# Last four k steps of the output ordered by token half, sums of squares on GpSimd, and two more quads with seven products in the ssm branch

## The chip, the core and the metric

The kernel runs on one core of a Trainium2 chip. The metric is the device time of one execution in microseconds (us). The core has five engines with instruction streams of their own: TensorE (PE, the matmuls), VectorE (DVE), ScalarE (ACT), GpSimd (POOL) and SyncE (SP), which here only issues transfers. Each engine executes its stream in the order in which it is written; semaphores make one wait for another.

## The reference

A hybrid layer on 256 tokens of width 2048, batch 1, in float32:

- `hn = rms_norm(x)`, then one wide projection `hn @ w_in` that is split into q, k, v, the gates, and the inputs of a state space branch (ssm).
- an attention branch with 16 heads and three dilated windows, gated, times `w_attn_branch`
- an ssm branch: a short causal convolution, a chunked scan, a gate and a norm give `y` (256 x 4096), which is multiplied with `w_ssm_branch` (4096 x 2048)
- `merged = sigmoid(g_a) * (o_a @ w_attn_branch) + sigmoid(g_s) * (y @ w_ssm_branch)`, then `x + merged @ w_out` and a last rms norm over each token's 2048 values.

The change touches two of the products, `y @ w_ssm_branch` and `merged @ w_out`, and the last norm.

## The kernel before

**Matmuls.** Each float32 operand is split into a high part (h) and a low part (l), and a product of two is made of three matmuls that add up in one bank of PSUM: high by high, high by low, low by high. Such a triple is one `triple` in `gemm_pair` (lines 375 to 378). All weights arrive as units of 128 x 1024 from one array, `wall`, in the order of use: 480 loads of 512 KB on SP's queue, into four buffers (`w`). For each unit ScalarE copies the high part (L220) and DVE subtracts to get the low part (L221); h and l have four buffers each.

**gemm_pair** (lines 361 to 444) makes a product of all 256 tokens with 1024 columns of a weight. Tokens lie in two halves (i = 0, 1) of 128 and columns in two halves (c = 0, 1) of 512, so there are four accumulators, es[2i + c], of one PSUM bank each. The loop runs over *quads*: a quad is two k tiles of 128 (so 2 x 2 blocks of x by 2 x 2 blocks of the weight). A plain quad takes eight triples: for both k, both i, both c. For the quads listed in `S_QUADS` a Strassen-like scheme takes seven triples in their place. It needs

- four combinations of the weight blocks, made on DVE (t13 at L421, w at L426 and L427) and each split again (L414 on ScalarE, L415 on DVE): in all, 7 DVE operations where a plain quad has 2;
- combinations of the blocks of x, made by `turn_x` (lines 341 to 359): DVE adds and subtracts (L347, L349 to L352) in a scratch tile and splits the results into high (L228, ScalarE) and low parts (L230, DVE). These are made once for a quad and used by both halves of the columns;
- four more banks, `prods` (pp in the profile), whose sums over all such quads are combined at the end by `fold` (L451 to L456) and added to the accumulators.

The second half of the columns (c = 2) uses the eight banks with the roles exchanged (`swap`): its accumulators take the banks of the first half's prods, its prods those of the first half's accumulators.

**The ssm product** (lines 789 to 805) has 16 quads for each half of the columns. Ahead of each half, the listed quads that have no turned x yet are turned; the scratch tile of `turn_x` has the tag "tmp" with one buffer, and the same tag holds the four 128 x 512 blocks into which the first half's fold and merge (L804, L805) write. Each half is handed to the scheduler in this order: turns, quads, fold, merge. In the first half 3, 7, 9, 13 are quads with seven products, in the second 3, 5, 7, 9, 11, 13.

**The output product** (lines 920 to 946) has 8 quads for each half of the columns; 3 and 5 have seven products. In the last quad (7) of each half the eight triples are sorted by accumulator; in all other plain quads they are sorted by k. After the second half, `fold` and two additions (L931) bring the prods into `fin`; then for each token half i and each block c = 2, 3 of 512 columns DVE adds the accumulator (L937), ScalarE squares with a running sum (L938), and DVE multiplies with the norm's weight (L939). For c = 2 DVE sums the three row sums so far and adds the epsilon (L941, L942); for c = 3 POOL adds the fourth (L944) and takes the power -0.5 (L945). Then the four blocks of each token half are scaled with that factor (L951 on ScalarE, L953 on DVE) and stored (L955).

**The order on each engine** is not the order of the source: a scheduler with a model of the engines' times orders the instructions before the program is built, and chooses which buffer of a tag is taken. So an edit in one place moves instructions around it.

Of the kernel before, what the change touches and what calls it, by code (L numbers as in the profile page):

```python
# [12 lines left out]
ALU = mybir.AluOpType  # L13
# [9 lines left out]
EPS = 1e-6  # L23
KT = D // P
# [12 lines left out]
GS_BEFORE = {0: (0, 1), 4: (2,)}  # L37
NEG = -1.0e30
S_QUADS = {
    ("ssm", 0): (3, 7, 9, 13), ("ssm", 2): (3, 5, 7, 9, 11, 13),  # L40
    ("v", 0): (4, 6), ("v", 2): (2, 4, 6), ("ga", 2): (2, 4, 6),
    ("out", 0): (3, 5), ("out", 2): (3, 5),
}
# [127 lines left out]
def hybrid_block(ctx: ExitStack, tc: tile.TileContext, wall, xt, x, pk_d, cst_d, fw_d, out):  # L171
# [39 lines left out]
    def unit(n, shape):  # L211
        if n not in loaded:
            load(n)
        w = loaded.pop(n)
        h = stream.tile([P, UNIT], F32R, name=f"h{n}", tag="h", bufs=H_BUFS)
        l = stream.tile([P, UNIT], F32R, name=f"l{n}", tag="l", bufs=H_BUFS)
        cuts = (0, UNIT // 2, UNIT) if n < N_FINE else (0, UNIT)
        with tc.high_priority(L_AHEAD) if n >= KT // UB else nullcontext():
            for a, b in zip(cuts, cuts[1:]):
                ac.activation(h[:, a:b], w[:, a:b], AF.Copy)  # L220
                ve.tensor_tensor(l[:, a:b], w[:, a:b], h[:, a:b].bitcast(F32), ALU.subtract)  # L221
        if n in on_unit:
            on_unit.pop(n)(h[:, 0:1].bitcast(F32))
        k, m = shape
        return h.rearrange("p (k m) -> p k m", k=k), l.rearrange("p (k m) -> p k m", k=k)
# [132 lines left out]
        split(s[:, spare:], sx[:, 0], sx[:, 1])  # L358
        return parts

    def gemm_pair(tag, x_of, n_kt, sxs, swap, extra={}):

        name = f"{tag[0]}{tag[1]}"
        quads = S_QUADS[tag]
        n_q = n_kt // 2
        first = FIRST[tag]
        tags = ("g", "g", "g", "g"), ("m1", "m1", "m2", "m2")
        e_tags, p_tags = tags[::-1] if swap else tags  # L370

        def banks(ts, s):
            return [bank(t, 4 if t == "g" else 2, f"{s}_{name}_{n}") for n, t in enumerate(ts)]

        def triple(acc, xh, xl, h, l, start, stop):
            pe.matmul(acc, xh, h, start=start, stop=False)  # L376
            pe.matmul(acc, xh, l, start=False, stop=False)  # L377
            pe.matmul(acc, xl, h, start=False, stop=stop)  # L378

        es = banks(e_tags, "ps")  # L380
        prods = []
        for q in range(n_q):
            tick()
            if q in extra:
                extra[q]()
            ks = [x_of(2 * q + k) for k in range(2)]
            a = [[(x[:, i * P : (i + 1) * P], x[:, S + i * P : S + (i + 1) * P]) for x in ks] for i in range(2)]
            n = first + 2 * q
            if q not in quads:
                hls = [unit(n + k, (2, 512)) for k in range(2)]  # L390
                steps = [(k, i, c) for k in range(2) for i in range(2) for c in range(2)]
                if q == n_q - 1:
                    steps.sort(key=lambda e: e[1:])
                for k, i, c in steps:
                    h, l = hls[k]
                    triple(
                        es[2 * i + c], *a[i][k], h[:, c], l[:, c],
                        start=(q == 0 and k == 0), stop=(q == n_q - 1 and k == 1),
                    )
                continue  # L400
            if not prods:
                prods = banks(p_tags, "pp")
            for m in (n, n + 1):
                if m not in loaded:
                    load(m)
            wa, wb = loaded.pop(n), loaded.pop(n + 1)

            def hl(where, suffix, tags, bufs):
                return [
                    where.tile([P, UNIT], F32R, name=f"{t}{suffix}{n}", tag=t, bufs=bufs) for t in tags  # L410
                ]

            def part(src, h, l):
                ac.activation(h, src, AF.Copy)  # L414
                ve.tensor_tensor(l, src, h.bitcast(F32), ALU.subtract)  # L415

            two = lambda t: t.rearrange("p (k m) -> p k m", k=2)
            with tc.high_priority(L_AHEAD):
                t13 = mul.tile([P, UNIT], F32, name=f"t13_{n}", tag="t13", bufs=1)
                b12 = wb[:, :512].unsqueeze(1).to_broadcast([P, 2, 512])  # L420
                ve.tensor_tensor(two(t13), b12, two(wa), ALU.subtract)  # L421
                ha, la = hl(stream, "a", "hl", H_BUFS)
                part(wa, ha, la)
                hc, lc = hl(stream, "c", "hl", H_BUFS)
                part(wb[:, 512:], hc[:, :512], lc[:, :512])
                ve.tensor_tensor(wb[:, :512], wa[:, 512:], t13[:, :512], ALU.subtract)  # L426
                ve.tensor_tensor(wb[:, 512:], wb[:, 512:], wb[:, :512], ALU.subtract)  # L427
                ht, lt = hl(mul, "t", ("ht", "lt"), 2)
                part(t13, ht, lt)
                hu, lu = hl(mul, "u", ("ht", "lt"), 2)  # L430
                part(wb, hu, lu)
            sx = sxs[q]
            lo, hi = slice(0, 512), slice(512, 1024)
            go, end = q == quads[0], q == quads[-1]
            for acc, x, h, l, cs, own in (
                (prods[0], a[0][0], ha, la, lo, True),
                (es[1], sx[3], ha, la, hi, False),
                (es[0], a[0][1], hc, lc, lo, False),
                (prods[1], sx[0], ht, lt, lo, True),
                (prods[3], sx[1], ht, lt, hi, True),  # L440
                (prods[2], sx[2], hu, lu, lo, True),
                (es[2], a[1][1], hu, lu, hi, False),
            ):
                triple(acc, *x, h[:, cs], l[:, cs], start=(own and go), stop=(own and end))
        return es, prods
# [343 lines left out]
    with tc.tile_pool(name="xp", bufs=1) as xp:  # L789
        sxs = {}  # L790
        for c in (0, 2):
            for q in S_QUADS[("ssm", c)]:
                if q not in sxs:
                    temp = xp.tile([P, 4, 512], F32, name=f"sxt_y{q}", tag="tmp", bufs=1)
                    sxs[q] = turn_x(xp, 6, temp, two_kts(yT[q // 8], q % 8), 1)
            es, prods = gemm_pair(
                ("ssm", c), lambda kt: yT[kt // 16][:, kt % 16, :], 2 * KT, sxs, c == 2,
                {2: scale_gate} if c == 0 else {},
            )
            tmp = xp.tile([P, 4, 512], F32, name=f"tmp{c}", tag="tmp", bufs=1)  # L800
            dst = [tmp[:, n] for n in range(4)]
            fold(prods, dst)
            for d, e, g in zip(dst, es, blocks(th_s, c)):
                ve.tensor_tensor(d, e, d, ALU.add)  # L804
                ve.tensor_tensor(g, g, d, ALU.mult)  # L805
# [87 lines left out]
    with tc.tile_pool(name="fin", bufs=2) as fp:  # L893
# [29 lines left out]
        for c0 in (0, 2):  # L923
            for n, q in enumerate(S_QUADS[("out", c0)]):
                if q not in sxs:
                    sxs[q] = turn_x(fp, 2, spare[:, 4 + 2 * n : 6 + 2 * n], two_kts(mT, q))
            es, prods = gemm_pair(("out", c0), lambda kt: mT[:, kt, :], KT, sxs, c0 == 2)
            fold(prods, [spare[:, n] for n in range(4)])
            for i in range(2):
                fc = fin[:, i, c0 * 512 : c0 * 512 + 1024]  # L930
                ve.tensor_tensor(fc, fc, spare[:, 2 * i : 2 * i + 2].rearrange("p n m -> p (n m)"), ALU.add)  # L931
            for i in range(2):
                f = fs[:, i, :8]
                for c, acc in zip((c0, c0 + 1), es[2 * i : 2 * i + 2]):
                    cs = slice(c * 512, (c + 1) * 512)
                    y = fp.tile([P, 512], F32, name=f"y{c}{i}", tag="y", bufs=2)
                    ve.tensor_tensor(y, fin[:, i, cs], acc, ALU.add)  # L937
                    ac.activation(acc, y, AF.Square, scale=float(D) ** -0.5, accum_out=f[:, c : c + 1])  # L938
                    ve.tensor_tensor(fin[:, i, cs], y, fw[:, cs], ALU.mult)  # L939
                    if c == 2:  # L940
                        ve.tensor_reduce(f[:, 4:5], f[:, 0:3], mybir.AxisListType.X, ALU.add)  # L941
                        ve.tensor_scalar(f[:, 5:6], f[:, 4:5], EPS, None, ALU.add)  # L942
                    if c == 3:
                        gp.tensor_tensor(f[:, 6:7], f[:, 3:4], f[:, 5:6], ALU.add)  # L944
                        gp.tensor_tensor(f[:, 7:8], f[:, 6:7], half[:, 0:1], ALU.pow)  # L945
# [43 lines left out]
```

## Time and profile before

| | |
|---|---|
| time, median of 3 runs | 1403.0 us (1402.68 to 1403.01) |
| the profiled execution | 1403.02 us |
| its span, first to last instruction | 1401.2 us |
| TensorE busy | 1387.2 us, 99% |
| DVE busy | 1063.7 us, 76% |
| ScalarE busy | 803.5 us, 57% |
| POOL busy | 15.8 us, 1% |
| ssm product | about 586 to 754 us |
| output product, second half, and what follows | up to the end |

A row of the timeline gives an instruction's start and length, its engine, its line, what it writes and reads, and in brackets how long the engine had been idle before it and what ended that. In the rows of matmuls (L376, L377, L378) `ps_` are the accumulators and `pp_` the prods. `ha`, `hc`, `htt` and `htu` are the high parts for a quad with seven products, `la`, `lc`, `ltt` and `ltu` the low parts, `sx` the turned blocks of x.

### The profile page before, as it was taken

What the parts mean: (1) busy time and instruction counts of PE and PEld (TensorE: products, weight loads), DVE (VectorE), ACT (ScalarE), POOL (GpSimd) and SP (SyncE); (2) the same over time, 40 slices, a digit from 0 to 9 for tenths busy, and PEclk for the clock granted to TensorE, in tenths of its full rate; (3) what the DMA queues carried; (4) which work ended last, traced back from release to release, by engine and by line L of the source; (5) the groups of instructions that cost most, each with busy time, mean ns of one, the idle gap of its engine ahead of it and who ended that gap; (6) DMA issues with size and microseconds to landing.
All of it is one profiled execution on the core that took longest, in us unless ns stands there. A gap on an engine that the chain in (4) does not pass through costs nothing.

```text
span 1401.2 us, 19822 instructions
## 1 busy us (share of the span) xinstructions
PE 1387.2 (99%) x7320; PEld 1179.5 (84%) x7320; DVE 1063.7 (76%) x1578; ACT 803.5 (57%) x1243; POOL 15.8 (1%) x66
## 2 busy tenths in 40 slices
PE   9999999999999999999999999999999999999997
PEld 7788888888888888888888888888888888888885
DVE  6988787786788787797988986666666656855897
ACT  7657577675667575665554554544454544534454
POOL 1000000000000000000000000000000000000000
PEclk9999999999999999999999999999999999999999
DMA  8666665666565655556566566655555557766564
GB/s 328 214 206 204 189 203 168 212 179 208 178 202 179 209 188 182 182 183 222 172 218 196 187 218 195 177 170 173 173 172 174 170 177 250 234 191 182 176 198 135
DMA packets 78209, 272.32 MB, mean 194 GB/s; under 512 B 8800, under 2 KB 9376, under 8 KB 77728
## 3 DMA queue, kind: packets, MB, share of 16 engines
q1 hardware_dynamic: 77392, 269.88, 61.3%
q8 instruction: 57, 0.93, 0.3%
q10 hardware_dynamic: 720, 1.18, 0.2%
q14 instruction: 40, 0.33, 0.1%
HBM read 268.86 MB, written 2.16 MB: 193 GB/s over the span
## 4 chain that ended last, share of the span: by engine, by line
PE 97%; DVE 2%; DMA 0%; issue 0%; SPq 0%; ACT 0%; POOLq 0%; DVEq 0%; POOL 0%
PE ps_zs L259 8%; PE ps_xs L259 8%; PE ps_za L259 4%; PE ps_k L259 4%; PE ps_q L259 4%; PE ps_zs L260 4%; PE ps_xs L260 4%; PE ps_ssm L376 3%; PE ps_ssm L377 3%; PE ps_ssm L378 3%; PE ps_q L260 2%; PE ps_k L260 2%; PE ps_za L260 2%; PE ps_attn L337 2%; PE ps_attn L335 2%; PE ps_attn L336 2%
## 5 line engine op out<-in xcount | busy, mean ns | idle before, releaser
L221 DVE TENSOR_TENSOR l<-w,h 128x1024 fp32r<-128x1024 f32 (+1 forms) x440 | 532.5, 1214 | 260.8 <-ACT h L220 258.1
L220 ACT ACTIVATE h<-w 128x1024 fp32r<-128x1024 f32 (+1 forms) x440 | 461.4, 1051 | 452.5 <-issue 95.5
L259 PE MATMUL ps_zs<-XT,h 128*128 128x512 f32 x496 | 176.2, 397 | 0.0
L259 PE MATMUL ps_xs<-XT,h 128*128 128x512 f32 x496 | 175.0, 395 | 0.0
L260 PE MATMUL ps_zs<-XT,l 128*128 128x256 f32 x496 | 139.4, 281 | 0.0
L260 PE MATMUL ps_xs<-XT,l 128*128 128x256 f32 x496 | 138.8, 280 | 0.0
L259 PEld LDWEIGHTS ps_zs<-XT,h 128*128 128x128 f32 x496 | 93.1, 188 | 22.7 <-issue 1.2
L259 PEld LDWEIGHTS ps_xs<-XT,h 128*128 128x128 f32 x496 | 93.0, 188 | 21.6
L260 PEld LDWEIGHTS ps_zs<-XT,l 128*128 128x128 f32 x496 | 93.6, 189 | 0.1
L260 PEld LDWEIGHTS ps_xs<-XT,l 128*128 128x128 f32 x496 | 93.6, 189 | 0.0
L259 PE MATMUL ps_q<-XT,h 128*128 128x512 f32 x256 | 92.4, 404 | 0.0
L259 PE MATMUL ps_za<-XT,h 128*128 128x512 f32 x256 | 89.7, 394 | 0.0
L259 PE MATMUL ps_k<-XT,h 128*128 128x512 f32 x256 | 89.7, 394 | 0.0
L260 PE MATMUL ps_q<-XT,l 128*128 128x256 f32 x256 | 71.3, 278 | 0.0
L260 PE MATMUL ps_k<-XT,l 128*128 128x256 f32 x256 | 71.0, 278 | 0.0
L260 PE MATMUL ps_za<-XT,l 128*128 128x256 f32 x256 | 71.0, 278 | 0.0
L377 PE MATMUL ps_ssm<-l,yT 128*128 128x512 f32 x176 | 68.6, 390 | 0.0
L378 PE MATMUL ps_ssm<-h,yT 128*128 128x512 f32 x176 | 68.2, 389 | 0.0
L376 PE MATMUL ps_ssm<-h,yT 128*128 128x512 f32 x176 | 62.9, 390 | 0.0
L259 PEld LDWEIGHTS ps_za<-XT,h 128*128 128x128 f32 x256 | 48.0, 188 | 11.3
L259 PEld LDWEIGHTS ps_k<-XT,h 128*128 128x128 f32 x256 | 48.0, 188 | 11.3
L259 PEld LDWEIGHTS ps_q<-XT,h 128*128 128x128 f32 x256 | 48.1, 188 | 10.9
(453 smaller groups left out, 2905.8 us busy)
## 6 DMA issues: line engine op xcount, KB each, us to landing
w<-in_wall SPq DMA_DIRECT2D x480, 512.0 KB, 3.7
acb<-acum_d SPq DMA_DIRECT2D x32, 256.0 KB, 3.5
th_s<-in_x SPq DMA_DIRECT2D x4, 512.0 KB, 8.0
vth<-in_x SPq DMA_DIRECT2D x1, 2048.0 KB, 9.5
early<-in_xt SPq DMA_DIRECT2D x7, 256.0 KB, 7.0
fw<-in_fw SPq DMA_DIRECT2D x1, 1024.0 KB, 8.2
out<-vth SPq DMA_DIRECT2D x4, 256.0 KB, 3.0
out<-vth ACTq DMA_DIRECT2D x4, 256.0 KB, 3.3
```

Source lines behind the costliest of these rows:

```text
L220: ac.activation(h[:, a:b], w[:, a:b], AF.Copy)
L221: ve.tensor_tensor(l[:, a:b], w[:, a:b], h[:, a:b].bitcast(F32), ALU.subtract)
L259: pe.matmul(acc, h[:, kk, :], m, start=(kt == 0), stop=False)
L260: pe.matmul(acc[:, S:], l[:, kk, :], m[:, :S], start=False, stop=(kt == KT - 1))
L335: pe.matmul(accs[i], xh, h[:, kk], start=(kt == 0), stop=False)
L336: pe.matmul(accs[i], xh, l[:, kk], start=False, stop=False)
L337: pe.matmul(accs[i], xl, h[:, kk], start=False, stop=(kt == KT - 1))
L376: pe.matmul(acc, xh, h, start=start, stop=False)
L377: pe.matmul(acc, xh, l, start=False, stop=False)
L378: pe.matmul(acc, xl, h, start=False, stop=stop)
```

## The change

Three edits. Two more quads of the ssm product use the seven products: 5, 7, 9, 11, 13 in the first half of the columns and 1, 3, 5, 7, 9, 11, 13 in the second, with seven buffers for turned x where there were six. In the second half of the output product the last two quads (6 and 7) are issued together, sorted by accumulator: `close=2` makes quad 6 only prepare its operands. And the sums for c = 2 in the last norm go from one reduction and one addition on DVE to three small operations on POOL.

```diff
-    ("ssm", 0): (3, 7, 9, 13), ("ssm", 2): (3, 5, 7, 9, 11, 13),
+    ("ssm", 0): (5, 7, 9, 11, 13), ("ssm", 2): (1, 3, 5, 7, 9, 11, 13),
...
-    def gemm_pair(tag, x_of, n_kt, sxs, swap, extra={}):
+    def gemm_pair(tag, x_of, n_kt, sxs, swap, extra={}, close=1):
...
             if q not in quads:
-                hls = [unit(n + k, (2, 512)) for k in range(2)]
-                steps = [(k, i, c) for k in range(2) for i in range(2) for c in range(2)]
+                ready = [] if q <= n_q - close else ready
+                ready += [(a, k, *unit(n + k, (2, 512))) for k in range(2)]
+                if n_q - close <= q < n_q - 1:
+                    continue
+                steps = [(e, i, c) for e in ready for i in range(2) for c in range(2)]
                 if q == n_q - 1:
-                    steps.sort(key=lambda e: e[1:])
-                for k, i, c in steps:
-                    h, l = hls[k]
+                    steps.sort(key=lambda s: s[1:])
+                for e, i, c in steps:
+                    ae, k, h, l = e
                     triple(
-                        es[2 * i + c], *a[i][k], h[:, c], l[:, c],
-                        start=(q == 0 and k == 0), stop=(q == n_q - 1 and k == 1),
+                        es[2 * i + c], *ae[i][k], h[:, c], l[:, c],
+                        start=(q == 0 and k == 0), stop=(q == n_q - 1 and e is ready[-1]),
                     )
                 continue
...
-                    sxs[q] = turn_x(xp, 6, temp, two_kts(yT[q // 8], q % 8), 1)
+                    sxs[q] = turn_x(xp, 7, temp, two_kts(yT[q // 8], q % 8), 1)
...
-            es, prods = gemm_pair(("out", c0), lambda kt: mT[:, kt, :], KT, sxs, c0 == 2)
+            es, prods = gemm_pair(("out", c0), lambda kt: mT[:, kt, :], KT, sxs, c0 == 2, {}, 2 if c0 else 1)
...
-                        ve.tensor_reduce(f[:, 4:5], f[:, 0:3], mybir.AxisListType.X, ALU.add)
-                        ve.tensor_scalar(f[:, 5:6], f[:, 4:5], EPS, None, ALU.add)
+                        gp.tensor_tensor(f[:, 4:5], f[:, 0:1], f[:, 1:2], ALU.add)
+                        gp.tensor_tensor(f[:, 4:5], f[:, 4:5], f[:, 2:3], ALU.add)
+                        gp.tensor_scalar(f[:, 5:6], f[:, 4:5], EPS, None, ALU.add)
```

With it the scheduler writes another order for the ssm product on TensorE, DVE and ScalarE, and for the tail. The order of the loads on SP's queue is the same as before.

## The prediction

> **What bounds the kernel now.** First the page: its span, the busy shares and the chain that ended last.
>
> ```profile
> span 1401.2 us, 19822 instructions
> PE 1387.2 (99%) x7320; PEld 1179.5 (84%) x7320; DVE 1063.7 (76%) x1578; ACT 803.5 (57%) x1243; POOL 15.8 (1%) x66
> PE 97%; DVE 2%; DMA 0%; issue 0%; SPq 0%; ACT 0%; POOLq 0%; DVEq 0%; POOL 0%
> ```
>
> The chain is TensorE for 97% of the span. The 2% on VectorE (DVE) lie at the start and in the tail. TensorE has almost no waits left to remove, so time can only go by issuing fewer matmuls or by a shorter tail; and any new wait of TensorE is added in full. This profiled execution took 1403.02 us, 1.8 more than its span; the median of the three runs is 1403.0. So I add changes of the span straight to 1403.0.
>
> Next the stretches in which the ssm branch runs (columns: busy us and instruction count of each engine, then the granted clock, the DMA share and GB/s): its first half, its second half, and the hand-over between them.
>
> ```profile
> 600.00:671.00 71.00, 71.00 (x316) 58.84 (x316) 59.08 (x81) 40.42 (x45) 2.62 (x1) 1.00 0.65 205
> 671.00:755.00 84.00, 84.00 (x372) 69.56 (x372) 75.48 (x90) 46.80 (x52) 0.00 (x0) 1.00 0.63 203
> 664.00:688.00 24.00, 24.00 (x107) 19.88 (x106) 21.41 (x31) 11.45 (x14) 0.00 (x0) 1.00 0.52 169
> ```
>
> TensorE never stops there, but DVE works 59.08 of 71, 75.48 of 84 and 21.41 of 24 us. Every quad with seven products takes matmuls from TensorE and gives DVE more to do, so the question is whether DVE can still deliver in time.
>
> Last the tail, in order of time:
>
> ```profile
> 1384.94 2.35 DVE L931 TENSOR_TENSOR vth<-vth,spare 128x1024 f32<-128x1024 f32 x2
> 1387.33 0.39 PE L378 MATMUL ps_out<-h,mT 128*128 128x512 f32 x1
> 1387.75 0.69 DVE L937 TENSOR_TENSOR y<-vth,ps_out 128x512 f32<-128x512 f32 x1 [0.46 <-PE ps_out L378]
> ...
> 1391.41 0.39 PE L378 MATMUL ps_out<-h,mT 128*128 128x512 f32 x1
> 1391.83 0.88 DVE L953 TENSOR_SCALAR vth<-vth,fs 128x512 f32<-128x512 f32 x2
> 1392.62 0.68 DVE L937 TENSOR_TENSOR y<-vth,ps_out 128x512 f32<-128x512 f32 x1
> 1393.48 0.60 ACT L938 ACTIVATE ps_out<-y 128x512 f32<-128x512 f32 x1 [0.93 <-DVE y L937]
> 1394.02 0.19 ACT L938 ACTIVATION_READ_ACCUMULATOR ps_out<-y 128x1 f32 x1
> 1394.28 0.15 DVE L942 TENSOR_SCALAR fs<-fs 128x1 f32<-128x1 f32 x1
> 1394.57 0.19 POOL L944 TENSOR_TENSOR fs<-fs 128x1 f32<-128x1 f32 x1 [2.99 <-DVE fs L942]
> 1394.84 0.56 POOL L945 TENSOR_TENSOR fs<-fs,half 128x1 f32<-128x1 f32 x1
> 1395.43 1.28 DVE L953 TENSOR_SCALAR vth<-vth,fs 128x512 f32<-128x512 f32 x3 [1.00 <-POOL fs L945]
> ```
>
> The matmul at 1387.33 is the last of accumulator 0, and 18 steps later, at 1391.41, the last of accumulator 3 starts: 4.08 / 18 = 0.2267 us a step (the 0.39 of a row overlaps the next). DVE reads accumulator 0 at 1387.75, so a result can be read 0.42 us after its last matmul starts. Accumulator 3 can be read at 1391.83 and is read at 1392.62; from there the add, the square, GpSimd (POOL) and the last scaling follow one another.
>
> **Part 1: fewer matmuls.** Each quad changed has seven triples in place of eight, so 3 matmuls less. One more quad in each half: 2 x 3 x 0.2267 = **1.36 us less**. TensorE is the bound, so this is worth its full size unless a wait takes it back.
>
> **Part 2: the hand-over between the halves.** Before, the second half starts with three plain quads; its first quad with seven products starts at 687.83.
>
> ```profile
> 659.95 0.39 PE L378 MATMUL pp_ssm<-htu,sx 128*128 128x512 f32 x1
> 671.51 0.39 PE L376 MATMUL ps_ssm<-h,yT 128*128 128x512 f32 x1
> 687.83 0.39 PE L376 MATMUL pp_ssm<-ha,yT 128*128 128x512 f32 x1
> 660.98 0.69 DVE L453 TENSOR_TENSOR tmp<-pp_ssm,tmp 128x512 f32<-128x512 f32 x1
> 661.70 0.69 DVE L454 TENSOR_TENSOR tmp<-pp_ssm,tmp 128x512 f32<-128x512 f32 x1
> 662.50 0.69 DVE L455 TENSOR_TENSOR tmp<-tmp 128x512 f32<-128x512 f32 x1
> 663.23 0.69 DVE L456 TENSOR_TENSOR tmp<-tmp 128x512 f32<-128x512 f32 x1
> 672.32 0.68 DVE L805 TENSOR_TENSOR th_s<-th_s,tmp 128x512 f32<-128x512 f32 x1
> 672.92 1.22 DVE L221 TENSOR_TENSOR l<-w,h 128x1024 fp32r<-128x1024 f32 x1
> 674.06 0.69 DVE L805 TENSOR_TENSOR th_s<-th_s,tmp 128x512 f32<-128x512 f32 x1
> 677.53 0.29 DVE L349 TENSOR_TENSOR sxt_y<-sxt_y 128x128 f32<-128x128 f32 x1
> 677.73 0.29 DVE L350 TENSOR_TENSOR sxt_y<-sxt_y 128x128 f32<-128x128 f32 x1
> 680.89 0.51 ACT L228 ACTIVATE sx<-sxt_y 128x384 fp32r<-128x384 f32 x1
> ```
>
> The second half's first matmul is at 671.51. Start to start, a DVE operation of 128x512 costs 0.60 (672.32 to 672.92), one of 128x1024 1.14 (672.92 to 674.06), one of 128x128 0.20 (677.53 to 677.73), and links of the fold that wait for each other 0.72 to 0.80 (660.98, 661.70, 662.50).
>
> Changed, the second half's first quad with seven products is quad 1, 5.4 us (24 steps) in. Its turned blocks of x (turn_x) use the one buffer "tmp" that the first half's fold and merge use too, and quad 1, unlike the quads 5 and 11 that were turned here before, is needed at once. In the scheduler's new order the last matmul of product bank 2 of the first half stands 30 steps before the second half's start; that start comes 3 steps earlier, at 671.51 - 0.68 = 670.83, so it is at 670.83 - 30 x 0.2267 = 664.03, and DVE can begin the fold at 664.45. From there to the last 128x128 step of quad 1's turn (L352) DVE has, with none to spare: 17 operations of 128x512 (4 of the fold, 8 of the merge at L804 and L805, the two combinations of quad 1's weights and one of quad 3's, one low part, the first sum of the turn), 10 of 128x1024 (2 differences, 8 low parts), 5 of 128x128: 17 x 0.60 + 10 x 1.14 + 5 x 0.20 = 22.6, and 0.4 for the fold's links: DVE is through at 687.5, and with the copy on ScalarE (0.51) the turned blocks are there at 688.0.
>
> TensorE has, from 664.03 up to the first matmul that reads them, 87 steps in that order, all that does not need them already put first: 664.03 + 87 x 0.2267 = 683.75. So it waits 688.0 - 683.75 = 4.3 us. A second count: the low part of quad 1's combined weights (ltu) comes two operations of 128x512 or their like earlier, is ready near 686.4, and 9 matmuls stand between it and that point: 688.4, a wait of 4.7. I take **4.6 us of waits**, split over several places of quads 1 and 2 as each operand arrives. Below it is bounded by zero, where DVE would run ahead; above by one weight load more in that chain:
>
> ```profile
> w<-in_wall SPq DMA_DIRECT2D x480, 512.0 KB, 3.7
> ```
>
> w of quad 3 can only be fetched when a buffer that quad 1 or 2 holds comes free, and the difference of quad 3 stands inside the DVE chain; if its 3.7 us end up in front, the wait is some 2 us more (7 at most). Behind quad 3 I find 1 us or more to spare again: a pair of quads costs TensorE 45 steps = 10.2 us and DVE 3 x 0.60 + 6 x 1.14 = 8.6. The loads of w keep their number and their order on SP's queue, which is passed by nothing.
>
> **Part 3: the first half.** Its quads with seven products were 3, 7, 9, 13; they become 5, 7, 9, 11, 13, each with its turn there. A quad with seven products costs DVE 4 x 1.14 + 3 x 0.60 = 6.4, a plain one 2 x 1.14 = 2.3, a turn 2.1 (one 128x512, five 128x128, and one 128x384 at some 0.5): 4.1 + 2.1 more, 59.08 + 6.2 = 65.3 of 70.3 us. With a turn a pair costs DVE 8.6 + 2.1 = 10.7 against 10.2, so it loses half a us a pair over three pairs; counting on from 603, I find it 0 to 1 us ahead at its tightest, quad 8. I take 0.2 us of waits, bounds 0 and 1.5. The other stages have the same instructions.
>
> **Part 4: the tail.** The last two quads are now ordered by accumulator: in the new order the last matmuls of accumulators 0, 1, 2 stand 25, 22 and 11 steps before that of 3 (before 18, 12, 6), so they can be read at 1386.2, 1386.8 and 1389.3. DVE is free of L931 at 1384.94 + 2 x 1.14 = 1387.2, and starts there instead of at 1387.75. Then two adds and two multiplications bring it to 1389.65, accumulator 2's add to 1390.25. The second square is done at 1389.4; POOL's sum and power took 1394.21 (end of the accumulator's row) to 1395.43 = 1.2, with 0.07 in it for L942, so the first rows' factor is there at 1390.4 to 1390.5. Three scalings (0.40 each) and a multiplication are queued ahead of the add of accumulator 3: it starts at 1392.2 to 1392.3, not 1392.62. From there before took 2.81 to the last scaling, of which L942 and a late ScalarE are 0.2. So the end comes **0.7 us earlier**. It can't be more than 0.79 + 0.36 = 1.15 (accumulator 3 is there at 1391.83). And less, to 0.3 later, if POOL's first factor is late, because the three scalings now wait ahead of that add. The sums on POOL: two more instructions of 0.19, for accumulators 0 to 2, done while accumulator 3 still runs; that work hides them, and without it they would cost some 0.5 us. The last two quads keep four h buffers until the end; the loads of w are all done by then, and no matmul needs a new one.
>
> **Sum:** -1.36 + 4.6 + 0.2 - 0.7 = +2.7 us: **1405.7 us**, 0.2% above 1403.0. Under 0.2% (2.8 us) either way a measurement of this kernel can hardly be told from no change, so my forecast lies at that bound.
>
> **Rivals.** *The wait is not there (ends on the other side).* If DVE's chain at the hand-over is shorter or begins earlier, the wait shrinks; the change becomes a gain once it is under 2.1 us, and with none the time is 1403.0 - 1.36 - 0.7 = 1400.9. For it: in 664 to 688 before, DVE still had time to wait for ScalarE:
>
> ```profile
> L221 DVE TENSOR_TENSOR l<-w,h 128x1024 fp32r<-128x1024 f32 x7 | 8.6, 1223 | 2.2 <-ACT h L220 2.2
> ```
>
>  Against: 23 us of DVE work stand against 19.7 us of matmuls, by steps seen in rows. Chance 0.14, most of it with part of the wait left.
>
> *A lower clock.* The granted clock falls when TensorE rests:
>
> ```profile
> 1388.00:1392.00 4.00, 3.79 (x17) 2.82 (x15) 3.93 (x9) 2.23 (x7) 0.74 (x2) 1.00 0.00 0
> 1392.00:1396.00 4.00, 0.00 (x0) 0.00 (x0) 3.00 (x9) 1.85 (x4) 0.75 (x2) 0.81 0.71 260
> 1396.00:1401.20 5.20, 0.00 (x0) 0.00 (x0) 0.71 (x2) 0.15 (x1) 0.00 (x0) 0.50 0.56 205
> 56.00:60.00 4.00, 3.02 (x13) 2.17 (x12) 4.00 (x10) 2.22 (x3) 0.00 (x0) 1.00 0.44 131
> ```
>
> A mean of 0.81 over 1392 to 1396 means about 2.5 us at 1.00 and then 0.50: some 2.7 us after the last matmul. About 1 us of rest in 56 to 60 left it at 1.00. If the 4.6 us came as one gap, matmuls would for some 2.7 us run at half speed: +1.35, 1407.1. My waits are split into pieces under 2 us, so chance 0.05. The Trainium skill, "TensorE: Matmul & The Clock Gate", Part 1, says that an idle window of about 3.4 us halves the clock and a busy one restores it; the rows agree on the half and suggest a slightly shorter time. By its window the loss would be about 1.7, 1407.4, as an estimate.
>
> *DVE is late in the first half too*, or a weight load joins the chain: 2 us more, 1407.7. Chance 0.14.
>
> *The tail does not move* (POOL late, or the scalings ahead of the add): 0.7 back, 1406.4. Chance 0.12.
>
> **How the numbers follow.** Forecast 0.55 (1404.4 to 1406.6, about half of it beyond +2.8), the rivals as above. Slower by over 0.2%: 0.27 + 0.05 + 0.13 + 0.07 = 0.52. Within 0.2%: 0.45. Faster by over 0.2% needs more than 2.8 us, and all gains at their bounds make 2.5: 0.03. The range leaves out the rival without a wait below and a load in the chain above: 1402.2 to 1407.6.
>
> **What would show it.** In the changed profile: waits of TensorE for DVE or ScalarE on ps_ssm and pp_ssm between 676 and 689, some 4 to 5 us in sum; DVE without a gap from 664 to 688; the first half ending 0.7 earlier, the second over 2 later than before; the last L953 group some 0.7 nearer to TensorE's end. Wrong: no such wait (part 2 falls), a wait before 664 (part 3), or the last add still 0.8 behind accumulator 3 (part 4).

## The result, and the profile after

The changed kernel takes **1408.15 us** (median of 5 runs, 1407.88 to 1408.79) against 1403.0 us before (1402.68 to 1403.2, 5 runs): ratio 1.0037, 95% interval 1.0026 to 1.0048. It is 5.1 us slower; the forecast was 1405.7 (1402.2 to 1407.6). The direction came out, the size did not.

The lines of the changed helper are 3 higher here: L418 splits the combined weights (L415 before), L424, L429 and L430 combine them, L456 to L459 are the fold, L807 and L808 the merge. In the tail L940 is the add of an accumulator, L945 to L949 are POOL's, L957 the scaling.

First the page: its span, the busy shares and the chain that ended last.

```profile
span 1406.3 us, 19843 instructions
PE 1389.0 (99%) x7314; PEld 1179.2 (84%) x7314; DVE 1073.1 (76%) x1591; ACT 804.6 (57%) x1249; POOL 17.4 (1%) x72
PE 94%; DVE 3%; DMA 1%; issue 1%; ACT 0%; SPq 0%; POOL 0%; POOLq 0%; DVEq 0%; ACTq 0%
```

TensorE issued the 6 matmuls less (7314, not 7320), and yet the span is 5.1 longer; the chain has gone from 97% on TensorE to 94%, and DMA, which had 0%, has 1%. That last figure is the first hint of what the forecast missed.

Where TensorE waited in the ssm product, from the list of its waits (us in total, times, longest):

```profile
PE pp_ssm L377 <- DVE la L418: 1.8, 1, 1.8
PE ps_ssm L377 <- DVE l L221: 1.4, 1, 1.4
PE ps_ssm L377 <- DVE ltu L418: 0.3, 1, 0.3
```

All three are new, and all are for VectorE. The stretches of the hand-over show when (columns as in the prediction):

```profile
676.00:680.00 4.00, 2.20 (x10) 1.20 (x8) 4.00 (x7) 1.06 (x1) 0.00 (x0) 1.00 0.25 60
680.00:684.00 4.00, 2.63 (x8) 1.86 (x7) 4.00 (x6) 1.08 (x2) 0.00 (x0) 0.52 0.65 203
684.00:688.00 4.00, 4.00 (x12) 2.78 (x10) 4.00 (x6) 1.35 (x2) 0.00 (x0) 0.63 0.56 174
```

TensorE executed 10, 8 and 12 matmuls where 4 us hold 17 to 18 at full speed, VectorE never rested, and the granted clock fell to about a half in between. VectorE's timeline over the hand-over:

```profile
663.11 1.23 DVE L221 TENSOR_TENSOR l<-w,h 128x1024 fp32r<-128x1024 f32 x1 [2.37 <-ACT h L220]
664.26 0.69 DVE L456 TENSOR_TENSOR tmp<-pp_ssm,tmp 128x512 f32<-128x512 f32 x1
...
668.70 1.23 DVE L424 TENSOR_TENSOR t<-w,w 128x1024 f32<-128x1024 f32 x1 [2.30 <-DMA w<-in_wall]
...
683.86 0.68 DVE L347 TENSOR_TENSOR sxt_y<-yT 128x512 f32<-128x512 f32 x1
...
687.14 1.22 DVE L418 TENSOR_TENSOR ltu<-w,htu 128x1024 fp32r<-128x1024 f32 x1
...
689.28 0.28 DVE L352 TENSOR_TENSOR sxt_y<-sxt_y 128x128 f32<-128x128 f32 x1
...
690.75 0.69 DVE L347 TENSOR_TENSOR sxt_y<-yT 128x512 f32<-128x512 f32 x1
```

The fold begins at 664.26 (forecast 664.45). But then VectorE rests for 2.30 us until the weights of quad 1 have landed, and only from 668.70 on is there no gap. Quad 1's turn takes the scratch tile at 683.86, after the last merge, and is through at 689.6; that of quad 3 begins at 690.75. The same stretch on TensorE, from its timeline, and the one issue on SP's queue that the rest at 668.70 was for:

```profile
676.53 0.39 PE L376 MATMUL ps_ssm<-h,yT 128*128 128x512 f32 x1
678.72 0.50 PE L377 MATMUL pp_ssm<-la,yT 128*128 128x512 f32 x1 [1.80 <-DVE la L418]
...
681.66 0.79 PE L377 MATMUL ps_ssm<-l,yT 128*128 128x512 f32 x1 [1.37 <-DVE l L221]
...
688.41 0.50 PE L377 MATMUL ps_ssm<-ltu,yT 128*128 128x512 f32 x1 [0.26 <-DVE ltu L418]
...
690.59 0.39 PE L376 MATMUL ps_ssm<-ha,sx 128*128 128x512 f32 x1
```

```profile
664.36 0.33 SPq L209 DMA_DIRECT2D w<-in_wall  x1
```

The first matmul that reads turned x starts at 690.59; without waits it could be reached at 683.75, as the prediction counted. So it comes **6.84 us** late, not 4.6. The list above has 3.4 us of this as waits; eleven steps of 0.43 us at the lower clock (682.25 to 686.95), where 0.2267 is usual, make 2.2 more; the rest is in slower steps next to the waits (as 0.33 us from 678.72 to 679.05). These pieces are not a sum of causes: what sets the whole is when `ltu` is ready, as the comparison with experiment 2 shows further below. The load was issued at 664.36, the moment the last plain unit's low part (663.11 + 1.23 = 664.34) gave its buffer back, and VectorE's rest ends 4.34 us after that issue.

Already ahead of the ssm product, executions differ by some tenths of a us: its first matmul is at 585.90 here and at 586.10 before, and between 585.28 and 586.68 in the experiments. Counted from that matmul the delay is 7.04 us. Where small differences between two profiles matter below, they are counted from there.

Last the tail:

```profile
1394.26 0.35 POOL L945 TENSOR_TENSOR fs<-fs 128x1 f32<-128x1 f32 x1 [32.47 <-ACT ps_out L941]
1394.70 0.55 POOL L946 TENSOR_SCALAR fs<-fs 128x1 f32<-128x1 f32 x1
1395.33 0.19 POOL L948 TENSOR_TENSOR fs<-fs 128x1 f32<-128x1 f32 x1
1395.60 0.57 POOL L949 TENSOR_TENSOR fs<-fs,half 128x1 f32<-128x1 f32 x1
1396.21 1.28 DVE L957 TENSOR_SCALAR vth<-vth,fs 128x512 f32<-128x512 f32 x3 [0.45 <-POOL fs L949]
1396.88 0.39 PE L378 MATMUL ps_out<-h,mT 128*128 128x512 f32 x1
1398.00 0.68 DVE L940 TENSOR_TENSOR y<-vth,ps_out 128x512 f32<-128x512 f32 x1
1400.47 1.28 DVE L957 TENSOR_SCALAR vth<-vth,fs 128x512 f32<-128x512 f32 x3 [1.06 <-POOL fs L949]
```

From the last matmul's start to the last scaling it is 1400.47 - 1396.88 = 3.59 us, before 1395.43 - 1391.41 = 4.02: 0.43 gained. The last matmul itself starts at 1396.88, not 1391.41: 5.47 later, which is 6.84 of delay less 1.36 of matmuls. So the sum of the trace is -1.36 + 6.84 - 0.43 = 5.05, and the spans differ by 5.1.

### The profile page after: what moved, and what is told of

It reads as the page before. It is cut to its first block, busy times and chain, and to the rows that moved or that the text cites. A ratio compares the mean times of both kernels' runs of the same rounds, so it can differ in the third digit from the quotient of the medians.

```text
span 1406.3 us, 19843 instructions
## 1 busy us (share of the span) xinstructions
PE 1389.0 (99%) x7314; PEld 1179.2 (84%) x7314; DVE 1073.1 (76%) x1591; ACT 804.6 (57%) x1249; POOL 17.4 (1%) x72
## 4 chain that ended last, share of the span: by engine, by line
PE 94%; DVE 3%; DMA 1%; issue 1%; ACT 0%; SPq 0%; POOL 0%; POOLq 0%; DVEq 0%; ACTq 0%
PE ps_zs L259 8%; PE ps_xs L259 8%; PE ps_k L259 4%; PE ps_za L259 4%; PE ps_q L259 4%; PE ps_zs L260 4%; PE ps_xs L260 4%; PE ps_ssm L377 3%; PE ps_ssm L376 3%; PE ps_ssm L378 3%; PE ps_q L260 2%; PE ps_za L260 2%; PE ps_k L260 2%; PE ps_attn L337 2%; PE ps_attn L335 2%; PE ps_attn L336 2%
## 5 line engine op out<-in xcount | busy, mean ns | idle before, releaser
L221 DVE TENSOR_TENSOR l<-w,h 128x1024 fp32r<-128x1024 f32 (+1 forms) x436 | 526.7, 1212 | 258.2 <-ACT h L220 255.6
L220 ACT ACTIVATE h<-w 128x1024 fp32r<-128x1024 f32 (+1 forms) x436 | 456.3, 1050 | 443.3 <-issue 97.0
L377 PE MATMUL ps_ssm<-l,yT 128*128 128x512 f32 x160 | 63.2, 396 | 1.4 <-DVE l L221 1.4
L378 PE MATMUL ps_ssm<-h,yT 128*128 128x512 f32 x160 | 63.2, 396 | 0.0
L376 PE MATMUL ps_ssm<-h,yT 128*128 128x512 f32 x160 | 54.4, 393 | 0.0
```

## The experiments

Every run stands beside runs of the kernel before on the same chip; their median was 1402.78 us for experiments 1 to 4, 1403.01 for 5 to 8, 1403.04 for 9 to 12 and 1403.01 for 13 and 14. Diffs are against the changed kernel unless said otherwise.

### 1 to 3: one part of the change alone

Experiment 1 has the tail's two edits and the old quads; 2 has the new quads and the old tail; 3 has the new quads in the first half only, and the old tail.

```diff
-    ("ssm", 0): (5, 7, 9, 11, 13), ("ssm", 2): (1, 3, 5, 7, 9, 11, 13),
+    ("ssm", 0): (3, 7, 9, 13), ("ssm", 2): (3, 5, 7, 9, 11, 13),         # 1
+    ("ssm", 0): (5, 7, 9, 11, 13), ("ssm", 2): (3, 5, 7, 9, 11, 13),     # 3
...
-                        gp.tensor_tensor(f[:, 4:5], f[:, 0:1], f[:, 1:2], ALU.add)
+                        ve.tensor_reduce(f[:, 4:5], f[:, 0:3], mybir.AxisListType.X, ALU.add)   # 2, 3; close=1 too
```

> The tail's edits alone (order of the last two quads, sums on GpSimd), the ssm product as before. By the theory that the tail's chain is simply 0.4 us closer to TensorE's end (1400.47 - 1396.88 = 3.59 in the changed kernel, 1395.43 - 1391.41 = 4.02 before): 1402.6, span 1400.8. By the rival that the tail costs something (GpSimd's small sums, 0.35 and 0.55 us in the changed kernel): 1403.0 or more.

> The ssm product's edit alone, the output product and the norm as before. By the theory that TensorE's waits at the hand-over are the whole loss: -1.36 + 6.9 = +5.5, so 1408.5, with waits of TensorE between 676 and 689 only. By the rival that part of the loss comes from the tail: 1407 or less.

> Only the first half of the ssm product is changed (5, 7, 9, 11, 13; second half 3, 5, 7, 9, 11, 13 as before). By the theory that quad 1 makes the wait: no wait of TensorE, 3 matmuls less: 1403.0 - 0.7 = 1402.3. By the rival that the five quads in a row already leave VectorE behind: a wait before 671 or in quad 3 of the second half, 1404 or more.

Measured: 1 took 1402.22 us (0.9996, 0.9987 to 1.0005), 2 took 1407.95 (1.0036, 1.0022 to 1.0050), 3 took 1402.22 (0.9996, 0.9987 to 1.0005). The whole loss is the ssm product's (2). The intervals of 1 and 3 include no change, so their gains of about half a us rest on the profiles: in 1 it is 3.58 us from the last matmul's start to the last scaling (before 4.02), and in 3 no wait of TensorE lies in the ssm product and the last matmul comes 0.69 us earlier, counted from the ssm product's start, for three matmuls less, which are worth 0.68.

### 4: the second half alone

```diff
-    ("ssm", 0): (5, 7, 9, 11, 13), ("ssm", 2): (1, 3, 5, 7, 9, 11, 13),
+    ("ssm", 0): (3, 7, 9, 13), ("ssm", 2): (1, 3, 5, 7, 9, 11, 13),
```

with the tail as before.

> Only the second half of the ssm product is changed (first half 3, 7, 9, 13 as before; 1, 3, 5, 7, 9, 11, 13 in the second, so that 1, 5 and 11 are turned at the hand-over). By the theory that quad 1 makes the wait: -0.7 + 5 to 7 us of waits between 676 and 690: 1407 to 1409.5. By the rival that both halves are needed for the loss: 1404 or less.

Measured: 1404.42 us (1.0013, 1.0004 to 1.0022), well under what the theory gave and a little over the rival's 1404. Quad 1 in the second half does cost, but the large loss needs the first half's new quads as well. Rows of its timelines on VectorE and TensorE:

```profile
665.88 1.22 DVE L424 TENSOR_TENSOR t<-w,w 128x1024 f32<-128x1024 f32 x1 [2.18 <-DMA w<-in_wall]
679.30 0.68 DVE L347 TENSOR_TENSOR sxt_y<-yT 128x512 f32<-128x512 f32 x1
686.15 0.50 PE L376 MATMUL ps_ssm<-ha,sx 128*128 128x512 f32 x1
```

The same chain begins 2.8 us earlier (665.88, not 668.70) and the first reader comes 4.4 earlier. Experiments 6 to 8 ask which part of the first half does that.

### 5: the turns out of the chain

```diff
+            def turns(qs):
+                for q in qs:
...
-                {2: scale_gate} if c == 0 else {},
+                {2: scale_gate, 14: lambda: turns(S_QUADS[("ssm", 2)])} if c == 0 else {},
```

> As the changed kernel, but the turned blocks of x of quads 1 and 3 of the second half are made at quad 14 of the first half, before the fold takes their buffer. Theory (VectorE's chain of work at the hand-over sets the wait of 6.8 us; every VectorE operation in it counts): some 2 x 2.1 = 4.2 us of VectorE go out of the chain, the wait falls to 2 to 3.5 us, 1403.5 to 1405.5 us against 1408.15. Rival (the weight loads of quads 1 to 3 set it; VectorE's work between them is hidden by them): the turns were beside the loads, wait 5.5 us or more, 1406.8 to 1408.2. Second rival (VectorE is late at quad 14 already): the wait moves ahead of 671 and the sum of waits stays near 6.

Measured: **1402.16 us** (0.9995, 0.9985 to 1.0004), 6.0 less than the changed kernel and below the range that was expected. Its rows on VectorE and TensorE:

```profile
668.75 1.23 DVE L424 TENSOR_TENSOR t<-w,w 128x1024 f32<-128x1024 f32 x1
675.46 0.39 PE L376 MATMUL ps_ssm<-ha,sx 128*128 128x512 f32 x1
683.91 1.22 DVE L418 TENSOR_TENSOR ltu<-w,htu 128x1024 fp32r<-128x1024 f32 x1
```

The weights of quad 1 come as late as in the changed kernel (668.75), and still the wait has gone. Two things went with the turn: `ltu` is started 3.2 us earlier (683.91, not 687.14; 2.6 of it counted from the ssm product's start, 585.28 here), and TensorE can read turned x from 675.46 on, so it has other matmuls to do while `ltu` is made. That is more than the 4.2 us of operations that were counted for it: a late turn also keeps every matmul behind it out of reach.

### 6 to 8: which quads of the first half

```diff
+    ("ssm", 0): (3, 7, 9, 11, 13), ("ssm", 2): (1, 3, 5, 7, 9, 11, 13),   # 6
+    ("ssm", 0): (3, 5, 7, 9, 11),  ("ssm", 2): (1, 3, 5, 7, 9, 11, 13),   # 7
+    ("ssm", 0): (5, 7, 9, 13),     ("ssm", 2): (1, 3, 5, 7, 9, 11, 13),   # 8
```

> As the changed kernel, but the first half's five quads are 3, 7, 9, 11, 13: the first half still ends with 9, 11, 13, and quad 3 is turned in the first half already, so only quad 1's turn is left at the hand-over. Theory (VectorE's chain): one turn, 2.1 us, less, wait 4.7 us, 1406.0 (1405.3 to 1406.7). Rival (how late the first half ends decides, through the release of weight buffers): as the changed kernel, 1407.5 to 1408.5.

> As the changed kernel, but the first half's five quads are 3, 5, 7, 9, 11, so that it ends with four plain quads, and only quad 1's turn is left at the hand-over. Same number of matmuls. Theory (VectorE's chain, started earlier and one turn shorter): the wait is under 2.3 us (that of the run with 3, 7, 9, 13), 1401.3 to 1403.6. Rival (the second half's quads 1 and 3 cannot be had in time wherever the first half's lie, since their weights come too late): 1405 or more.

> As the changed kernel, but the first half has four quads, 5, 7, 9, 13 (0.68 us more of matmuls); against the earlier run with 3, 7, 9, 13 only quad 3's turn is added at the hand-over, against the changed kernel only quad 11 is taken out. Theory (VectorE's chain, each turn 2.1 us): 1404.4 - 0.5 (tail) + 2.1 = 1406.0 (1405.3 to 1406.7). Rival (lateness of the first half's end alone): 1403.9 (1403.4 to 1404.4).

Measured, with the start of L424 and L347 for quad 1 and of the first matmul that reads turned x:

| | first half | ssm starts | L424 | L347 | first reader | us | ratio (95%) |
|---|---|---|---|---|---|---|---|
| changed | 5 7 9 11 13 | 585.90 | 668.70 | 683.86 | 690.59 | 1408.15 | 1.0037 (1.0026 to 1.0048) |
| 2 (old tail) | 5 7 9 11 13 | 585.32 | 667.99 | 683.15 | 689.89 | 1407.95 | 1.0036 (1.0022 to 1.0050) |
| 6 | 3 7 9 11 13 | 586.22 | 668.76 | 683.93 | 690.65 | 1407.76 | 1.0034 (1.0021 to 1.0047) |
| 7 | 3 5 7 9 11 | 586.50 | 668.28 | 680.70 | 688.14 | 1405.75 | 1.0020 (1.0010 to 1.0029) |
| 8 | 5 7 9 13 | 585.85 | 667.77 | 680.06 | 687.51 | 1405.35 | 1.0018 (1.0009 to 1.0027) |
| 4 (old tail) | 3 7 9 13 | 585.78 | 665.88 | 679.30 | 686.15 | 1404.42 | 1.0013 (1.0004 to 1.0022) |

In 6 the theory missed: with quad 3 turned in the first half nothing changes. The rows say why: in the changed kernel the second turn begins at 690.75, behind the first reader, so it was never in the chain. Quad 11 was: 6 and 4 differ by it (and by the tail), and it moves L424 by 2.4 us and the first reader by 4.1, counted from the ssm product's start. In 7 the time is the rival's, and both the theory and the rival are half right. The half ends with four plain quads, and still quad 1's weights come hardly earlier (668.28; 1.0 us, counted from the ssm product's start): ScalarE makes the last plain high parts at TensorE's pace, as rows like these of experiment 7 tell, and their low parts give the buffers back.

```profile
664.57 1.06 ACT L220 ACTIVATE h<-w 128x1024 fp32r<-128x1024 f32 x1 [1.66 <-PE ps_ssm L378]
667.29 1.06 ACT L220 ACTIVATE h<-w 128x1024 fp32r<-128x1024 f32 x1 [1.66 <-PE ps_ssm L378]
```

What it gains is work in the chain: from L424 to L347 VectorE has 12.4 us to do, not 15.2, two low parts and one link of the fold less (2 x 1.14 + 0.60 = 2.9). 8 came out inside the theory's range, but not for the theory's reason: quad 3's turn begins at 688.09 there, behind the first reader at 687.51, so it is not in the chain. Against 4 the chain starts 1.8 us later though the first half has four such quads in both, so the places of these quads count and not only their number; what makes that difference was not traced. In all six the time follows the first reader: where it comes, the rest of the kernel starts.

### 9: the same number of matmuls, without quad 1

```diff
-    ("ssm", 0): (5, 7, 9, 11, 13), ("ssm", 2): (1, 3, 5, 7, 9, 11, 13),
+    ("ssm", 0): (5, 7, 9, 11, 13), ("ssm", 2): (3, 5, 7, 9, 11, 13, 14),
```

> As the changed kernel, with the same number of matmuls, but the second half's seven quads are 3, 5, 7, 9, 11, 13, 14: quad 1 is plain again, its turn is not needed at the hand-over, and quad 14 takes its place at the far end of the half. Theory (the loss is the place of the first quad with seven products, whose weights land at about 668.7 with some 20 us of VectorE work between them and the first matmul that reads turned x): no wait at the hand-over, 1401.2 plus at most 1 us for VectorE at quads 13 and 14: 1401.2 to 1402.2. Rival (seven quads in the second half are more than VectorE can carry, wherever they lie): 1404 or more.

Measured: **1401.23 us** (0.9986, 0.9977 to 0.9995). Its stretches at the hand-over, and of the end of the second half:

```profile
664.00:688.00 24.00, 24.00 (x108) 19.87 (x107) 22.80 (x32) 11.36 (x13) 0.00 (x0) 1.00 0.63 200
734.00:758.00 24.00, 24.00 (x108) 19.87 (x107) 20.07 (x24) 12.52 (x14) 0.00 (x0) 1.00 0.58 193
```

TensorE is busy all of the time. Seven such quads are not too many; the place of the first one is what costs. It is the version that beats both kernels, and its gain is the forecast's matmuls and the tail as measured, without the hand-over: -1.36 - 0.43 = -1.8, and 1403.04 - 1.8 = 1401.24. Its profile has both: from the ssm product's first matmul to the last matmul it is 803.94 us, before 805.31, and from there to the last scaling 3.60.

### 10 to 12: the tail, and other versions

Experiment 10 has the old second half and all else of the change. Experiment 11 has the old quads and of the tail only the order (`close=2`), with the sums on VectorE. Experiment 12 has 3, 7, 9, 11, 13 in the first half and turns quad 1 alone at quad 12 there, with the function of experiment 5.

```diff
+    ("ssm", 0): (5, 7, 9, 11, 13), ("ssm", 2): (3, 5, 7, 9, 11, 13),      # 10
...
+    ("ssm", 0): (3, 7, 9, 13), ("ssm", 2): (3, 5, 7, 9, 11, 13),          # 11
+                        ve.tensor_reduce(f[:, 4:5], f[:, 0:3], mybir.AxisListType.X, ALU.add)
...
+    ("ssm", 0): (3, 7, 9, 11, 13), ("ssm", 2): (1, 3, 5, 7, 9, 11, 13),   # 12
+                {2: scale_gate, 12: lambda: turns((1,))} if c == 0 else {},
```

> The two parts of the change that cost nothing: the first half with 5, 7, 9, 11, 13 and the tail as changed; the second half as before (3, 5, 7, 9, 11, 13). If parts add up: 1403.0 - 0.68 - 0.5 = 1401.8 (1401.2 to 1402.3). Rival (the later end of the first half's products delays quad 3 of the second half): 1402.5 or more.

> The ssm branch as before; of the tail's two edits only the order of the last matmuls, with the sums of squares on VectorE as before. From the last matmul's start to the last scaling the kernel before took 4.02 us and the changed one 3.59. Theory (the order brings all of the gain, and moving the sums to GpSimd delays the first factor by the 0.35 and 0.55 us that two of them took): 3.1 to 3.5 us, 1402.2 to 1402.6. Rival (the sums on GpSimd are what frees VectorE): 3.8 us or more, 1402.7 to 1403.1.

> A version that should beat both: first half 3, 7, 9, 11, 13 (so quad 3 is turned there), second half 1, 3, ..., 13, quad 1's turn made at quad 12 of the first half, tail as changed. All matmuls of the change are saved (-1.36), the tail's 0.5 too; the early turn takes the hand-over's wait away and puts only one turn, 2.1 us, on VectorE ahead of the fold. Theory: 1401.2 to 1402.2, at or below the run with both turns made early (1402.16). Rival (a weight load behind quad 3 makes the next wait): 1402.2 to 1403.0.

Measured: 10 took 1401.72 us (0.9991, 0.9982 to 1.0000), near the 1401.8 that the two harmless parts were expected to add up to; the interval just reaches no change. Experiment 11 took 1402.70 (0.9997, 0.9988 to 1.0006), with these rows in its tail:

```profile
1391.25 0.55 POOL L948 TENSOR_TENSOR fs<-fs,half 128x1 f32<-128x1 f32 x1
1391.45 0.39 PE L378 MATMUL ps_out<-h,mT 128*128 128x512 f32 x1
1392.30 0.68 DVE L940 TENSOR_TENSOR y<-vth,ps_out 128x512 f32<-128x512 f32 x1
1395.09 1.28 DVE L956 TENSOR_SCALAR vth<-vth,fs 128x512 f32<-128x512 f32 x3 [0.72 <-POOL fs L948]
```

From the last matmul to the last scaling it is 3.64 us, a little over the 3.1 to 3.5 expected, against 3.59 with the sums on POOL and 4.02 before. So the order brings nearly all of the tail's gain. The sums on POOL trade: with them the add of accumulator 3 starts 1.12 after the last matmul, here 0.85, and what follows it takes 2.47, here 2.79. These are spans of one profile each; the times (1402.22 in experiment 1, 1402.70 here) cannot tell the two apart.

Experiment 12 missed: 1402.67 (0.9996, 0.9987 to 1.0005), no better than experiment 5 and inside what its rival gave. Rows of its VectorE, TensorE and ScalarE:

```profile
682.09 0.68 DVE L347 TENSOR_TENSOR sxt_y<-yT 128x512 f32<-128x512 f32 x1
689.25 0.28 DVE L352 TENSOR_TENSOR sxt_y<-sxt_y 128x128 f32<-128x128 f32 x1
```

```profile
686.59 0.50 PE L376 MATMUL pp_ssm<-htt,yT 128*128 128x512 f32 x1 [0.36 <-ACT htt L417]
692.94 1.06 ACT L417 ACTIVATE ha<-w 128x1024 fp32r<-128x1024 f32 x1 [1.25 <-DMA w<-in_wall]
694.05 0.50 PE L376 MATMUL pp_ssm<-ha,yT 128*128 128x512 f32 x1 [0.35 <-ACT ha L417]
```

Quad 1's turn was gone, but the turn of quad 5, which nothing needs yet, now stands at the hand-over and among quad 3's weights, and TensorE loses 0.71 us there (0.36 + 0.35). Only the first of these waits can be the turn's, and that it is was not tried. The second is for a high part that ScalarE could make only once its weights had landed, the weight load behind quad 3 that the rival named; experiment 5, without that turn, has the same wait (0.48 us, at 694.77).

### 13 and 14: the weight load

Experiment 13 puts quad 1's two loads ahead of quad 0's on SP's queue and leaves all else; 14 does this together with the turns of experiment 5.

```diff
-                {2: scale_gate} if c == 0 else {},
+                {2: scale_gate} if c == 0 else {0: lambda: [load(FIRST[("ssm", 2)] + m) for m in (2, 3)]},
```

> As the changed kernel, but at the hand-over the two weight loads of quad 1 stand ahead of those of quad 0 on SP's queue; VectorE's operations and all matmuls are the same in kind and number. Theory (VectorE's chain to the first matmul that reads turned x began only when quad 1's second load landed, at 668.7, after 2.3 us of rest): the difference of quad 1's weights starts at about 664.3, right at the end of the last plain low part, the first reader comes 2 to 2.5 us earlier than 690.6, 1405.6 to 1406.3 us against 1408.15, which is what was forecast without a load in the chain. Rival (the load had cover elsewhere, another operand sets that reader): 1407.5 to 1408.5.

> Both at once: turns of quads 1 and 3 made at quad 14 of the first half, and quad 1's weight loads ahead of quad 0's. Theory: the hand-over's wait is gone already with the early turns (1402.16), what was left there is a weight load behind quad 3; earlier loads move it little: 1401.2 to 1402.2. Rival (quad 0's loads, now later, make TensorE wait): 1402.5 or more.

Measured: 13 took **1406.22 us** (1.0022, 1.0013 to 1.0032), 1.9 less than the changed kernel and within what the theory gave. Its rows on VectorE and TensorE:

```profile
666.04 1.23 DVE L424 TENSOR_TENSOR t<-w,w 128x1024 f32<-128x1024 f32 x1 [1.29 <-DMA w<-in_wall]
684.14 1.22 DVE L418 TENSOR_TENSOR ltu<-w,htu 128x1024 fp32r<-128x1024 f32 x1
685.27 0.69 DVE L347 TENSOR_TENSOR sxt_y<-yT 128x512 f32<-128x512 f32 x1
689.32 0.50 PE L376 MATMUL ps_ssm<-ha,sx 128*128 128x512 f32 x1 [0.26 <-ACT sx L228]
```

This execution began the ssm product at 586.68, 0.78 us later than that of the changed kernel. Counted from there the chain starts 3.4 us earlier, `ltu` 3.8 earlier and the first reader 2.05 earlier. That is less than `ltu` gained, because the new order puts the turn's start behind `ltu` (685.27, not 683.86), and now the turned x is last. So some 1.9 us of the 2.2 that the forecast lacked are shown to be this load, together with the order that the scheduler wrote around it. Experiment 14 took 1402.39 (0.9997, 0.9987 to 1.0006), a little over the range and not to be told from experiment 5: once the turns are out of the way, an earlier load buys nothing that these runs can show.

## Why the prediction was wrong

**Part 1 was right**: 7314 matmuls, and experiment 9 shows the 1.36 us in full (805.31 - 803.94 = 1.37).

**Part 2 is the step that failed, by its size.** The place, the cause (VectorE's chain up to quad 1's turn, behind the scratch tile) and the split into short waits came as written. The failing sentence is that from 664.45 on VectorE has its operations "with none to spare". It had 2.30 us to spare, at 666.4, because the first operation for quad 1 had no weights. Its count of VectorE's operations was exact (17, 10 and 5 from the fold to L352), so the rest is what was missing. `ltu` was ready at 688.36, not near 686.4, and the delay was 6.84, not 4.6. The prediction had a weight load only as an upper bound, with the wrong load: that of quad 3, whose difference stands without a gap in the changed kernel. Its 7 us at most and its rival at 1407.7, given 0.14, were the nearest to what came. What it did not do was ask, for the first operation of the chain that was not the fold's, when its buffer came free and add the load's time. Experiment 13 shows that load (1.9 us); experiment 5 shows that the turn was the larger lever all the same (6.0 us). The whole miss of 2.45 us is made up of 2.24 here and 0.27 in Part 4, less the 0.2 of Part 3 that did not come: 2.31.

**Part 3 was right about the first half and blind to what it hands on.** TensorE does not wait there, in the changed kernel or in experiment 3. But the fifth quad of the first half delays its last plain low part and with it quad 1's load: between experiments 4 and 6 it is 4.1 us at the first reader. A stage that is just in time was counted as free, though it passes its lateness on.

**Part 4** gained 0.43, not 0.7. The first factor was to be there 0.9 to 1.0 before the last matmul's start and came 0.7 before it (1396.21 against 1396.88), since two of POOL's three sums took 0.35 and 0.55 us, not the 0.19 of the row that they were priced by. The three scalings behind it then held the last add to 1.12 after that matmul, not 0.8 to 0.9.

**The rival of a lower clock** came to pass and cost nothing that shows. The one-us stretches of the changed kernel at the fall and at the return (the clock is the third figure from the end), and then the stretches of experiment 2:

```profile
680.00:681.00 1.00, 0.28 (x2) 0.00 (x0) 1.00 (x2) 0.00 (x0) 0.00 (x0) 0.58 0.70 254
...
686.00:687.00 1.00, 1.00 (x4) 0.71 (x3) 1.00 (x3) 0.00 (x0) 0.00 (x0) 0.51 0.53 217
687.00:688.00 1.00, 1.00 (x5) 0.46 (x3) 1.00 (x3) 0.31 (x1) 0.00 (x0) 1.00 0.12 49
```

```profile
676.00:680.00 4.00, 1.90 (x7) 0.78 (x5) 4.00 (x7) 1.06 (x1) 0.00 (x0) 1.00 0.27 63
680.00:684.00 4.00, 2.91 (x11) 1.91 (x11) 4.00 (x6) 1.79 (x2) 0.00 (x0) 1.00 0.65 215
684.00:688.00 4.00, 2.44 (x7) 1.08 (x7) 4.00 (x6) 0.64 (x2) 0.00 (x0) 1.00 0.40 119
```

A mean of 0.58 puts the fall at about 680.2, and the return is at 687.0. It fell though the longest gap between two matmuls was 2.2 us (676.53 to 678.72) and five matmuls stood behind it before the clock fell. Yet at 688.41 TensorE still waited for `ltu`, and VectorE had no gap, so a faster TensorE would only have waited longer. Experiment 2 shows this: it has the same ssm product, its clock stayed at 1.00, TensorE waited more (its list has another 0.94 us at 686.70), and the first reader came 104.57 us after the ssm product's start, in the changed kernel 104.69. The lower clock cost 0.1 us at most.

The Trainium skill, "TensorE: Matmul & The Clock Gate", Part 1, has the window run free of the kernel; windows of its 3.4 us that end at 680.2 and 687.0 would hold TensorE some 47% busy in the first case (an estimate by the page's figure) and all busy in the second. If the windows lay so, one that was half busy was enough for the fall, a share for which the page gives no figure; no row here shows where they lay.

Two things were not tried: a fifth weight buffer, which would issue quad 1's load earlier, and a second scratch tile, which would let the turn run beside the merge.

## What to carry to other kernels

Where one stage's first demanding step follows closely on another, write down for its first operations not only the engine's work but when each operand's buffer is released and its load lands; a chain starts at the latest of these. A preparation step that shares a scratch buffer with the stage before (here `turn_x` with the fold and merge) belongs ahead of that stage's end, or the step that needs it belongs later: moving the quad from 1 to 14 kept all six matmuls saved. A stage in which nothing waits can still be late for the next one, so test edits of two neighbouring stages together and apart.

## What was not expected of the hardware

Small operations on POOL do not have one price: additions of 128x1 took 0.19, 0.35 and 0.55 us in the rows above, with about 0.09 between one and the next. And the clock does not answer the same rests in the same way. It fell to one half after about 3.3 us in which TensorE had rested for 1.8 and worked for some 1.5, and it fell in experiment 6 too (a mean of 0.63 over 680 to 684). In experiment 2, with the same matmuls and nearly the same rests there (1.68 and 1.38 us, not 1.80 and 1.37), it stayed at 1.00, as it did in experiment 13, where TensorE was busy 12.89 of the 16 us from 676 to 692. What decided between them is not shown here.
